# Linear attention on one core: paired output stores, and a regrouped end of the kernel

## The chip, the core and the metric

The kernel runs on one core of a Trainium2 chip. The metric is the device time of one execution in microseconds (us). The kernel before was timed in four runs: 126.88, 127.28, 127.53 and 127.73 us, median 127.4 us. Device work on a core is done by TensorE (PE, with its weight loads shown apart as PEld), VectorE (DVE), ScalarE (ACT), GpSimd (POOL) and SyncE (SP); 16 DMA engines move data between HBM and SBUF, and they are given their work by POOL and SP here.

## What is computed

For each of 8 x 12 = 96 heads, with 512 rows of 64 numbers in float32:

```
Q_feat = max(0, Q) + 1;  K_feat = max(0, K) + 1
KV     = K_feat^T V                    (64 x 64 per head)
K_sum  = sum of K_feat over the rows   (64 per head)
out    = (Q_feat KV) / (Q_feat K_sum + 1e-10)
```

Three inputs of 12 MiB each are read and one output of 12 MiB is written, all in float32.

## The kernel before, in words

**Groups.** The 96 heads are cut into 12 groups of 8 heads (NG = 12, g = 0 to 11). Two groups in a row (0 and 1, 2 and 3, ...) make a pair. A group's output is 1 MiB, 8 KB in each of the 128 partitions. Groups 2 to 9 (`eights(g)`, L93) keep their Q rows in another order than groups 0, 1, 10 and 11: their outputs go to every second of a pair's eight output rows (L137), while the others go to four rows that follow each other. In HBM each partition's piece of one such row is a run of 2 KB, in both cases.

**Loads.** `load` (L104) and `load_q` (L115) are DMAs issued by POOL that read float32 and write bfloat16 into SBUF; `load_pair` (L124) issues K, V and Q of a whole pair, 1 MiB each in SBUF and 2 MiB each in HBM (Q of the last pair in two halves). Each of the three has two buffers (IN_BUFS = 2), so the load of a pair waits until the pair before the last has been used up. The first K goes through SP (L101).

**Work on a group.** `k_features` and `q_features` (DVE, L147) make max(x + 1, 1). `v_blocks` (L158) copies V into a block matrix, three quarters on DVE (L165) and one on ACT (L163). `keys_values` (L177) is 32 matmuls on PE (L184), whose result ACT copies to SBUF (L194, L195). `transposes` (L197) is 16 matmuls on PE into PSUM in two halves (L209); ACT copies each half to SBUF, save the second half of group 11, which DVE copies (L213, L214). `output(g)` (L216) has two halves h = 0 and 1. Each has 16 matmuls (L231) into two PSUM tiles of the pool `psum`, which has two buffers; so the eight matmuls on one tile wait until DVE has used up what lay in it. DVE then takes a reciprocal and one multiplication for each of the two tiles (L241, L242), which writes into the group's tile `o_sb`.

**Stores.** `o_sb` is a tile of one group, of six buffers (OUT_BUFS = 6, 48 KB in each partition). `store(g)` (L134) is one DMA of 1 MiB, issued by POOL, for groups 0 to 9; groups 10 and 11 go out from SP in two DMAs of 512 KB each, one for each half h (L143, L144).

**Order.** The schedule is written out by hand (L260 and on), and each engine does its instructions in that order. The loop over g = 0 to 10 does features, `output(g - 2)`, `keys_values(g)`, and stores group g - 3 (LAG = 3); the transposes of a group lie in its own iteration or the next. `load_pair` stands in the odd iterations 1, 3, 5 and 7, ahead of the store of that iteration. In iteration 10 the order on the engines is `k_features(10)`, `output(8)`, `v_blocks(10)`, `k_features(11)`, `v_blocks(11)`, `keys_values(10)`. After the loop come `q_features(10)`, `transposes(10)`, `q_features(11)`, `output(9)`, `keys_values(11)`, `transposes(11)`, `output(10)`, `output(11)`, and the stores of groups 8 to 11.

POOL's DMAs share eight semaphores in turn. A DMA therefore also waits until the one issued eight before it has landed. POOL and SP issue in order, so a DMA that waits holds back those behind it.

For short, K4 below is the K load of pair 4 (groups 8 and 9), S7 the store of group 7, S10a and S10b the two halves of group 10's, and S45 a store of groups 4 and 5 together.

Of the kernel before, what the change touches and what calls it, by code (L numbers as in the profile page):

```python
# [8 lines left out]
FP32 = mybir.dt.float32  # L9
BF16 = mybir.dt.bfloat16  # L10
ALU = mybir.AluOpType

BANK = 512
IN_BUFS = 2
OUT_BUFS = 6
LAG = 3


# [1 line left out]
def kernel(  # L20
# [21 lines left out]
    nc = tc.nc  # L42

    B, H, S, D = Q.shape
    P = 128
    C = 8
# [3 lines left out]
    NP = 4  # L50
    NG = NPAIR // NP
    D1 = D + 1
    W = 2 * D1

    def view(t, c):
        return t.flatten_outer_dims().rearrange("(n p c) d -> p n c d", p=P, c=c)
# [5 lines left out]
    o_dram = view(out, C)  # L62
# [6 lines left out]
    mid_pool = ctx.enter_context(tc.tile_pool(name="mid", bufs=2))  # L69
    out_pool = ctx.enter_context(tc.tile_pool(name="out_pool", bufs=OUT_BUFS))  # L70
    recip_pool = ctx.enter_context(tc.tile_pool(name="recip", bufs=4))
    psum_kva = ctx.enter_context(tc.tile_pool(name="psum_kva", bufs=2, space=bass.MemoryType.PSUM))
    psum = ctx.enter_context(tc.tile_pool(name="psum", bufs=2, space=bass.MemoryType.PSUM))
# [3 lines left out]
    NV = 4  # L77
# [5 lines left out]
    kva_diag = [kva_all[:, i] for i in range(NV)]  # L83
# [5 lines left out]
    qfs = {}  # L89
    qts = {}  # L90
    outs = {}

    def eights(g):  # L93
        return 2 <= g < NG - 2
# [4 lines left out]
    def load_first_k():  # L99
        k_raw = head_pool.tile([P, 2, C2, D], FP32, name="k_first")  # L100
        nc.sync.dma_start(out=k_raw, in_=k_dram[:, 0:2])  # L101
        raw["k", 0] = k_raw
# [29 lines left out]
                load("q", (g,))  # L132

    def store(g):  # L134
        o_sb = outs.pop(g)
        first = 2 * NP * (g // 2)
        o_to = o_dram[:, first + g % 2 : first + 2 * NP : 2] if eights(g) else o_dram[  # L137
            :, g * NP : g * NP + NP
        ]
        if g < NG - 2:  # L140
            nc.gpsimd.dma_start(out=o_to, in_=o_sb)  # L141
            return
        for h in range(2):  # L143
            nc.sync.dma_start(out=o_to[:, h:NP:2], in_=o_sb[:, h:NP:2])  # L144
# [13 lines left out]
    def v_blocks(g):  # L158
        v_raw = raw.pop(("v", g))
        for b in range(4):  # L160
            ps = slice(32 * b, 32 * b + 32)
            if b == 3:
                nc.scalar.copy(out=v_blk[g % 2][ps, b], in_=v_raw[ps])  # L163
            else:
                nc.vector.tensor_copy(out=v_blk[g % 2][ps, b], in_=v_raw[ps])  # L165
# [11 lines left out]
    def keys_values(g):  # L177
        kf = kfs.pop(g)
        sb = g % 2
        vb = v_all[:, 4 * sb : 4 * sb + 5]  # L180
        kva_ps = psum_kva.tile([P, 5, D], FP32, name="kva_ps")
        for c in range(C2):
            for n in range(2):
                nc.tensor.matmul(  # L184
                    kva_ps[64 * n : 64 * n + 64],
                    lhsT=kf[:, c, n, :],
                    rhs=vb[:, :, n, c, :],
                    start=(c == 0),
                    stop=(c == C2 - 1),
                )  # L190
        kva = kva_diag[g % NV]
        for n in range(2):
            ps = slice(64 * n, 64 * n + 64)
            nc.scalar.copy(out=kva[ps, :, n, 0:D], in_=kva_ps[ps, sb : sb + 4, :])  # L194
            nc.scalar.copy(out=kva[ps, :, n, D], in_=kva_ps[ps, 4 - 4 * sb, 0:4])  # L195

    def transposes(g):  # L197
        qf = qfs.pop(g)
        R, CC = qf.shape[1:3]
        if R == 4 and g % 2:  # L200
            qts[g] = qts[g - 1]
        else:
            qts[g] = mid_pool.tile([P, C, P, R], BF16, name=f"qt{R}")
        first = g % 2 * CC if R == 4 else 0
        for half in range(2):
            qt_ps = psum_qt.tile([P, CC // 2, R, P], BF16, name="qt_ps")
            for c in range(CC // 2):
                for r in range(R):
                    nc.tensor.transpose(  # L209
                        qt_ps[:, c, r], qf[:, r, half * CC // 2 + c, :, :], identity  # L210
                    )
            lo = first + half * CC // 2
            copy = nc.vector.tensor_copy if half and g == NG - 1 else nc.scalar.copy  # L213
            copy(out=qts[g][:, lo : lo + CC // 2], in_=qt_ps.rearrange("p c r q -> p c q r"))  # L214

    def output(g):  # L216
        qt = qts.pop(g)
        o_sb = out_pool.tile([P, NP, C, D], FP32, name="o_sb")
        for h in range(2):
            ops = [psum.tile([P, 2, BANK], FP32, tag="ps", name="o_ps") for _ in range(2)]  # L220
            for c in range(C):
                for j in range(2):
                    if eights(g):
                        b = 2 * (g % 2) + j
                        kva = kva_diag[(g // 2 * 2 + h) % NV]
                        q = slice(16 * (4 * h + b), 16 * (4 * h + b) + 16)
                    else:
                        b = 2 * h + j
                        kva = kva_diag[g % NV]
                        q = slice(32 * b, 32 * b + 32)  # L230
                    nc.tensor.matmul(  # L231
                        ops[c // 4][64 * j : 64 * j + 64, c // 2 % 2, (c % 2) * W : (c % 2) * W + W],
                        lhsT=qt[:, c, q, :],
                        rhs=kva[:, b],
                        start=True,
                        stop=True,
                    )
            for i in range(2):
                cells = ops[i][:, :, 0 : 2 * W].rearrange("p b (c n x) -> p b c n x", n=2, x=D1)
                recip = recip_pool.tile([P, 2, 2, 2, 1], FP32, name="recip")  # L240
                nc.vector.reciprocal(out=recip, in_=cells[:, :, :, :, D:D1])  # L241
                nc.vector.tensor_tensor(  # L242
                    out=o_sb[:, h:NP:2, 4 * i : 4 * i + 4].rearrange(
                        "p n (b c) d -> p b c n d", b=2
                    ),
                    in0=cells[:, :, :, :, 0:D],
                    in1=recip.to_broadcast([P, 2, 2, 2, D]),
                    op=ALU.mult,
                )
        outs[g] = o_sb  # L250

    def clear(first, split, end):
        t = v_all.rearrange("p b m c d -> p (b m c d)").bitcast(FP32)
        w = t.shape[1] // 9
        nc.vector.memset(t[:, first * w : split * w], 0.0)  # L255
        nc.scalar.copy(  # L256
            out=t[:, split * w : end * w], in_=zero.to_broadcast([P, (end - split) * w])
        )

    with tc.manual_schedule():  # L260
        nc.gpsimd.memset(zero, 0.0)
        load_first_k()
        load("v", (0,))
        load("q", (0,))
        for x in "kvq":
            load(x, (1,))
        nc.vector.memset(ones, 0.0)
        for b in range(4):
            nc.vector.memset(ones[32 * b : 32 * b + 32, b : b + 1], 1.0)  # L269
        clear(0, 3, 5)  # L270
        e = v_all[:, 4, :, :, 0:4].rearrange("p n c j -> p (n c) j")
        nc.vector.tensor_copy(out=e, in_=ones[:, None, :].to_broadcast([P, 2 * C2, 4]))
        make_identity(nc, identity)
        nc.gpsimd.memset(kva_all, 0.0)
        load_pair(1)
        clear(5, 7, 9)
        last = NG - 1
        for g in range(last):
            if g and not eights(g - 1):
                transposes(g - 1)  # L280
            elif eights(g) and g % 2:
                transposes(g - 1)
            k_features(g)
            if g < last - 1:
                v_blocks(g)
                if not eights(g):
                    q_features(g)
            if g >= 2:
                output(g - 2)
            if g == last - 1:  # L290
                v_blocks(g)
                k_features(last)
                v_blocks(last)
            if eights(g) and g % 2:
                transposes(g)
            if eights(g) and g % 2 == 0:
                q_features(g)
                q_features(g + 1)
            keys_values(g)
            if g % 2 and g // 2 + 2 < NG // 2:  # L300
                load_pair(g // 2 + 2)
            if g >= LAG:
                store(g - LAG)
        q_features(last - 1)
        transposes(last - 1)
        q_features(last)
        output(last - 2)
        keys_values(last)
        transposes(last)
        output(last - 1)  # L310
        output(last)
        for g in range(last - LAG, NG):
            store(g)
# [30 lines left out]
```

## Time and profile before

| | before |
|---|---|
| median of 4 runs | 127.4 us (126.88 to 127.73) |
| the profiled execution | 126.88 us |
| its span, from the first to the last instruction | 125.1 us |
| busy: DVE | 90.0 us (72% of the span) |
| busy: PE, ACT, POOL | 71.4, 60.4, 26.8 us |
| HBM read and written | 37.75 MB and 12.58 MB, 402 GB/s over the span |
| share of the 16 DMA engines' time: POOL's queue, SP's queue | 97.5%, 6.8% |
| TensorE clock granted, mean | 0.84 |

The profiled execution's own time is 126.88 us and its span 125.1 us; 1.78 us lie outside the span. The page of a profile gives the busy time of each engine, then the span in 40 slices of 3.13 us: a digit is the busy share of an engine in tenths, and the DMA row is the mean busy share of the 16 DMA engines. The row in GB/s counts what is written to the destination. A load writes half of the bytes that it reads, so 210 GB/s in a slice of loads and 420 GB/s in a slice of stores are the same rate on the HBM side. The chain that ended last is followed back from the last instruction. In the list of groups of instructions a row gives line, engine, operation, tiles, count, busy time, mean duration and the idle time ahead of it with what ended it.

### The profile page before, as it was taken

Reading aid. Unit: us, or ns where it says so; the run is one execution under the profiler, and the core shown is the slowest. Engines: PE = TensorE matmul, PEld = TensorE weight load, DVE = VectorE, ACT = ScalarE, POOL = GpSimd, SP = SyncE. Lnnn points to the kernel's source line nnn. Section 1 sums busy time; section 2 is a strip of 40 time slices with the busy share of each in tenths; the row PEclk is TensorE's granted clock in tenths of the full one; section 3 lists DMA queues with packets and bytes.
Section 4 is the critical chain, followed back from the end, with each engine's and each line's share of the span. In section 5 each row is a group of like instructions: output and inputs, shape, how many; then the busy total and the mean of one; then the engine's idle time right before and its main releaser. Section 6 shows DMA issues by size and latency. Waiting matters only on the chain.

```text
span 125.1 us, 2332 instructions
## 1 busy us (share of the span) xinstructions
PE 71.4 (57%) x960; PEld 54.2 (43%) x960; DVE 90.0 (72%) x189; ACT 60.4 (48%) x86; POOL 26.8 (21%) x39
## 2 busy tenths in 40 slices
PE   0004944920696848549594594069787169693720
PEld 0003544810565847438373463056576046472410
DVE  4897280207999899996999930799877996739950
ACT  7832095266009982866729542600895471732000
POOL 6991204000020370224302420203110200020000
PEclk9999997798559999967999959955899756999555
DMA  3999999999999999999999999999999999999993
GB/s 75 342 212 211 212 210 210 212 218 213 208 212 215 216 213 210 210 210 221 245 410 301 210 215 217 210 360 386 221 211 215 208 281 420 423 420 409 389 360 130
DMA packets 12362, 32.12 MB, mean 257 GB/s; under 512 B 576, under 2 KB 576, under 8 KB 12352
## 3 DMA queue, kind: packets, MB, share of 16 engines
q0 software_dynamic: 10992, 28.84, 97.5%
q1 hardware_dynamic: 1360, 3.15, 6.8%
q8 instruction: 7, 0.11, 0.3%
q14 instruction: 3, 0.02, 0.0%
HBM read 37.75 MB, written 12.58 MB: 402 GB/s over the span
## 4 chain that ended last, share of the span: by engine, by line
DMA 47%; DVE 20%; PE 18%; issue 5%; ACT 4%; POOL 2%; POOLq 0%; DVEq 0%
DMA v_raw<-in_V_dram 47%; PE kva_ps L184 12%; DVE o_sb L242 11%; DVE v_all L165 6%; PE qt_ps L209 3%; DVE recip L241 2%; PE o_ps L231 2%; ACT qt L214 2%; ACT v_all L163 2%; POOL v_raw L109 1%; ACT kva_all L194 1%; POOL q_raw L109 1%; DVE qt L214 0%; POOL k_raw L109 0%; ACT kva_all L195 0%
## 5 line engine op out<-in xcount | busy, mean ns | idle before, releaser
L184 PE MATMUL kva_ps<-v_all,kf 128*64 128x320 bf16 x384 | 39.4, 376 | 18.0 <-DVE v_all L165 14.5
L184 PEld LDWEIGHTS <-kf 128*64 128x64 bf16 x384 | 27.9, 139 | 26.2 <-DVE v_all L165 15.6
L231 PE MATMUL o_ps<-kva_all,qt 128*64 128x130 bf16 x384 | 20.2, 243 | 30.3 <-DVE o_sb L242 19.6
L165 DVE COPY v_all<-v_raw 32x2048 bf16<-32x2048 bf16 x36 | 26.2, 727 | 12.8 <-DMA v_raw<-in_V_dram 12.4
L242 DVE TENSOR_TENSOR o_sb<-o_ps,recip 128x512 f32<-128x512 f32 x48 | 33.2, 692 | 1.6
L231 PEld LDWEIGHTS <-qt 128*64 128x64 bf16 x384 | 14.0, 119 | 35.7 <-DVE o_sb L242 23.7
L194 ACT CAST kva_all<-kva_ps 64x256 bf16<-64x256 f32 x24 | 8.9, 371 | 39.5 <-PE kva_ps L184 39.4
L163 ACT COPY v_all<-v_raw 32x2048 bf16<-32x2048 bf16 x12 | 22.6, 1893 | 9.3 <-DMA v_raw<-in_V_dram 9.1
L214 ACT COPY qt<-qt_ps 128x1024 bf16<-128x1024 bf16 x23 | 22.2, 1015 | 3.6 <-PE qt_ps L209 3.3
L141 POOL DMA_DIRECT2D out_dram<-o_sb x10 | 8.3, 834 | 33.6 <-DVE o_sb L242 21.3
L209 PE MATMUL qt_ps<-identity,qf 128*128 128x128 bf16 x192 | 14.9, 240 | 0.0
L147 DVE TENSOR_SCALAR kf<-k_raw 128x1024 bf16<-128x1024 bf16 x22 | 8.6, 433 | 8.4 <-DMA k_raw<-in_K_dram 8.4
L209 PEld LDWEIGHTS <-qf 128*128 128x128 bf16 x192 | 12.7, 108 | 3.2 <-issue 1.7
L241 DVE RECIPROCAL recip<-o_ps 128x8 f32<-128x8 f32 x48 | 9.6, 200 | 3.4 <-PE o_ps L231 3.2
L109 POOL DMA_DIRECT2D k_raw<-in_K_dram x6 | 4.7, 779 | 31.0 <-DVE kf L147 24.7
L147 DVE TENSOR_SCALAR qf<-q_raw 128x1024 bf16<-128x1024 bf16 x24 | 9.0, 432 | 0.3 <-DMA q_raw<-in_Q_dram 0.3
L109 POOL DMA_DIRECT2D v_raw<-in_V_dram x7 | 5.4, 767 | 17.2 <-ACT v_all L163 16.8
L255 DVE MEMSET v_all<- 128x3072 f32 (+1 forms) x2 | 4.4, 2192 | 1.1 <-DVE ones L269 0.7
L195 ACT CAST kva_all<-kva_ps 64x4 bf16<-64x4 f32 x24 | 4.1, 169 | 0.0
L256 ACT COPY v_all<-zero 128x2048 f32<-128x2048 f32 x2 | 3.7, 1894 | 0.0
L109 POOL DMA_DIRECT2D q_raw<-in_Q_dram x4 | 2.9, 722 | 2.3 <-DMA k_raw<-in_K_dram 2.3
L119 POOL DMA_DIRECT2D q_raw<-in_Q_dram x4 | 3.1, 786 | 0.0
(14 smaller groups left out, 7.8 us busy)
## 6 DMA issues: line engine op xcount, KB each, us to landing
out_dram<-o_sb POOLq DMA_DIRECT2D x10, 1024.0 KB, 24.0
k_raw<-in_K_dram POOLq DMA_DIRECT2D x5, 1024.0 KB, 22.4
v_raw<-in_V_dram POOLq DMA_DIRECT2D x5, 1024.0 KB, 23.0
q_raw<-in_Q_dram POOLq DMA_DIRECT2D x4, 1024.0 KB, 26.0
q_raw<-in_Q_dram POOLq DMA_DIRECT2D x4, 512.0 KB, 21.6
out_dram<-o_sb SPq DMA_DIRECT2D x4, 512.0 KB, 3.9
k_first<-in_K_dram SPq DMA_DIRECT2D x1, 1024.0 KB, 5.0
v_raw<-in_V_dram POOLq DMA_DIRECT2D x2, 512.0 KB, 9.5
```

The source lines that it names most:

```text
L109: nc.gpsimd.dma_start(out=bufs[x, s][:, ms], in_=drams[x][:, 2 * groups[0] : 2 * groups[-1] + 2])
L141: nc.gpsimd.dma_start(out=o_to, in_=o_sb)
L147: nc.vector.tensor_scalar(out=dst, in0=src, scalar1=1.0, scalar2=1.0, op0=ALU.add, op1=ALU.max)
L163: nc.scalar.copy(out=v_blk[g % 2][ps, b], in_=v_raw[ps])
L165: nc.vector.tensor_copy(out=v_blk[g % 2][ps, b], in_=v_raw[ps])
L184: nc.tensor.matmul(kva_ps[64 * n : 64 * n + 64], lhsT=kf[:, c, n, :], rhs=vb[:, :, n, c, :], start=(c == 0), stop=(c == C2 - 1),)
L194: nc.scalar.copy(out=kva[ps, :, n, 0:D], in_=kva_ps[ps, sb : sb + 4, :])
L209: nc.tensor.transpose(qt_ps[:, c, r], qf[:, r, half * CC // 2 + c, :, :], identity)
L214: copy(out=qts[g][:, lo : lo + CC // 2], in_=qt_ps.rearrange("p c r q -> p c q r"))
L231: nc.tensor.matmul(ops[c // 4][64 * j : 64 * j + 64, c // 2 % 2, (c % 2) * W : (c % 2) * W + W], lhsT=qt[:, c, q, :], rhs=kva[:, b], start ...
L241: nc.vector.reciprocal(out=recip, in_=cells[:, :, :, :, D:D1])
L242: nc.vector.tensor_tensor(out=o_sb[:, h:NP:2, 4 * i : 4 * i + 4].rearrange("p n (b c) d -> p b c n d", b=2), in0=cells[:, :, :, :, 0:D], i ...
```

## The change

It has two parts.

1. **Stores.** One tile of the output pool now holds a pair: 16 KB in each partition, three buffers (OUT_BUFS = 3), the same 48 KB in all. Groups 0 to 7 are stored two by two, by one DMA of 2 MiB at the place where the odd group's store stood (`store`); the even group's call does nothing. Groups 8 to 11 are stored as before, from their part of a pair's tile. For groups 8 and 9 that part is every second row of the tile.

2. **The end.** `output` is split into `out_matmuls(g, h)` on PE and `norms(g, h)` on DVE. The first half of group 9's output matmuls moves into iteration 10, ahead of `v_blocks(10)`. After the loop, the first half of group 10's output (matmuls and norms) stands between `keys_values(11)` and `transposes(11)`; the second half follows the transposes. ACT makes both copies of group 11's transposes.

For each other group the instructions of an output are what they were.

```diff
-OUT_BUFS = 6
+OUT_BUFS = 3
...
     def store(g):
+        first = 2 * NP * (g // 2)
+        if g < NG - 4:
+            if g % 2:
+                nc.gpsimd.dma_start(
+                    out=o_dram[:, first : first + 2 * NP], in_=outs.pop((g // 2, "pair"))
+                )
+            return
         o_sb = outs.pop(g)
-        first = 2 * NP * (g // 2)
...
-            copy = nc.vector.tensor_copy if half and g == NG - 1 else nc.scalar.copy
-            copy(out=qts[g][:, lo : lo + CC // 2], in_=qt_ps.rearrange("p c r q -> p c q r"))
+            nc.scalar.copy(out=qts[g][:, lo : lo + CC // 2], in_=qt_ps.rearrange("p c r q -> p c q r"))
+
+    def out_matmuls(g, h):
+        if h == 0:
+            open_outputs(g)
+        qt = qts[g]
+        ops = [psum.tile([P, 2, BANK], FP32, tag="ps", name="o_ps") for _ in range(2)]
+        cells_of[g, h] = ops
...
+    def open_outputs(g):
+        if g % 2 == 0:
+            outs[g // 2, "pair"] = out_pool.tile([P, 2 * NP, C, D], FP32, name="o_sb")
+        pair = outs[g // 2, "pair"]
+        o_sb = pair[:, g % 2 : 2 * NP : 2] if eights(g) else pair[:, g % 2 * NP : g % 2 * NP + NP]
+        outs[g] = o_sb
+
+    def norms(g, h):
+        ops = cells_of.pop((g, h))
+        o_sb = outs[g]
...
     def output(g):
...
         for h in range(2):
+            out_matmuls(g, h)
+            norms(g, h)
...
             if g == last - 1:
+                out_matmuls(g - 1, 0)
                 v_blocks(g)
                 k_features(last)
                 v_blocks(last)
...
         q_features(last)
-        output(last - 2)
+        norms(last - 2, 0)
+        out_matmuls(last - 2, 1)
+        norms(last - 2, 1)
         keys_values(last)
+        out_matmuls(last - 1, 0)
+        norms(last - 1, 0)
         transposes(last)
-        output(last - 1)
+        out_matmuls(last - 1, 1)
+        norms(last - 1, 1)
         output(last)
```

The loops of `out_matmuls` and `norms` that are left out are those of `output` before, L221 to L237 and L238 to L249.

More of the change, by code (lines that the diff above doesn't have):

```diff
@@ L91 @@
     outs = {}
+    cells_of = {}
     def eights(g):
@@ L212, in transposes @@
             lo = first + half * CC // 2
-            copy = nc.vector.tensor_copy if half and g == NG - 1 else nc.scalar.copy
-            copy(out=qts[g][:, lo : lo + CC // 2], in_=qt_ps.rearrange("p c r q -> p c q r"))
+            nc.scalar.copy(out=qts[g][:, lo : lo + CC // 2], in_=qt_ps.rearrange("p c r q -> p c q r"))
[5 more added lines that the diff above has]
+        cells_of[g, h] = ops
+        for c in range(C):
+            for j in range(2):
+                if eights(g):
+                    b = 2 * (g % 2) + j
+                    kva = kva_diag[(g // 2 * 2 + h) % NV]
+                    q = slice(16 * (4 * h + b), 16 * (4 * h + b) + 16)
+                else:
+                    b = 2 * h + j
+                    kva = kva_diag[g % NV]
+                    q = slice(32 * b, 32 * b + 32)
+                nc.tensor.matmul(
+                    ops[c // 4][64 * j : 64 * j + 64, c // 2 % 2, (c % 2) * W : (c % 2) * W + W],
+                    lhsT=qt[:, c, q, :],
+                    rhs=kva[:, b],
+                    start=True,
+                    stop=True,
+                )
@@ new lines, in open_outputs @@
+    def open_outputs(g):
[7 more added lines that the diff above has]
+        o_sb = outs[g]
+        for i in range(2):
+            cells = ops[i][:, :, 0 : 2 * W].rearrange("p b (c n x) -> p b c n x", n=2, x=D1)
+            recip = recip_pool.tile([P, 2, 2, 2, 1], FP32, name="recip")
+            nc.vector.reciprocal(out=recip, in_=cells[:, :, :, :, D:D1])
+            nc.vector.tensor_tensor(
+                out=o_sb[:, h:NP:2, 4 * i : 4 * i + 4].rearrange(
+                    "p n (b c) d -> p b c n d", b=2
+                ),
+                in0=cells[:, :, :, :, 0:D],
+                in1=recip.to_broadcast([P, 2, 2, 2, D]),
+                op=ALU.mult,
+            )
@@ L216, in output @@
     def output(g):
-        qt = qts.pop(g)
-        o_sb = out_pool.tile([P, NP, C, D], FP32, name="o_sb")
         for h in range(2):
[L220 to L249, printed above, removed]
@@ L250, in output @@
-        outs[g] = o_sb
+            out_matmuls(g, h)
+            norms(g, h)
     def clear(first, split, end):
```

## The prediction, made before the changed kernel had run

> **What bounds the kernel now.** I read the page's slices first, because they show which engine has no holes.
>
> ```profile
> DVE  4897280207999899996999930799877996739950
> DMA  3999999999999999999999999999999999999993
> GB/s 75 342 212 211 212 210 210 212 218 213 208 212 215 216 213 210 210 210 221 245 410 301 210 215 217 210 360 386 221 211 215 208 281 420 423 420 409 389 360 130
> q0 software_dynamic: 10992, 28.84, 97.5%
> q1 hardware_dynamic: 1360, 3.15, 6.8%
> ```
>
> Every engine has holes but the DMA row: 9 in each slice from the second to the last but one. Where the rate is about 210 GB/s the queue loads (which is 420 on the HBM side), and where it is about 420 it stores. So the time looks like bytes over a rate, with 3 us at the start and 2 at the end. The chain of waits tells another story.
>
> ```profile
> DMA 47%; DVE 20%; PE 18%; issue 5%; ACT 4%; POOL 2%; POOLq 0%; DVEq 0%
> ```
>
> In order of time that chain runs from a V load into PE and DVE at about 79 us, and from there to the end only through compute. It holds because S11b, the last store, is issued the moment DVE has finished. It does not say that the store would have landed earlier if issued earlier. For that I read VectorE's and SP's timelines and the time from issue to landing, one issue at a time.
>
> ```profile
> 107.08 0.21 DVE L241 RECIPROCAL recip<-o_ps 128x8 f32<-128x8 f32 x1 [1.70 <-PE o_ps L231]
> ...
> 112.60 1.22 DVE L214 COPY qt<-qt_ps 128x1024 bf16<-128x1024 bf16 x1 [2.07 <-PE qt_ps L209]
> 113.74 0.20 DVE L241 RECIPROCAL recip<-o_ps 128x8 f32<-128x8 f32 x1
> ...
> 119.94 0.69 DVE L242 TENSOR_TENSOR o_sb<-o_ps,recip 128x512 f32<-128x512 f32 x1
> ```
>
> ```profile
> 115.53 0.38 SPq L144 DMA_DIRECT2D out_dram<-o_sb  x1
> ...
> 120.66 0.37 SPq L144 DMA_DIRECT2D out_dram<-o_sb  x1
> ```
>
> ```profile
> out_dram<-o_sb POOLq DMA_DIRECT2D x1, 1024.0 KB, 8.0
> ...
> out_dram<-o_sb SPq DMA_DIRECT2D x1, 512.0 KB, 4.5
> ...
> out_dram<-o_sb SPq DMA_DIRECT2D x1, 512.0 KB, 3.2
> ```
>
> The last three rows are S9 (issued at 110.82), S10a and S11b. Issue plus landing time, with the same view for the others, gives the landings: S4 106.3, S5 108.8, S6 111.3, S7 113.8, S8 116.3, S9 118.8, S10a 120.0, S10b 121.3, S11a 122.6, S11b 123.8. The step is 2.5 us for 1 MiB and 1.25 to 1.3 for 512 KB, without a gap down to the last one. The time from issue to landing shrinks from 27.0 to 3.2 us: each store waits in the queue, and S11b comes just as the queue runs out. **The DMA queue sets the end; compute reaches it at the same moment.** The last rows to read are stretches of the span; their last two columns are the DMA share and GB/s.
>
> ```profile
> 103.50:116.00 12.50, 9.20 (x146) 6.59 (x142) 8.47 (x20) 4.70 (x11) 0.75 (x1) 0.91 1.02 417
> 116.00:123.00 7.00, 2.60 (x34) 1.64 (x32) 4.46 (x11) 0.00 (x0) 0.00 (x0) 0.50 0.96 373
> 123.00:125.00 2.00, 0.00 (x0) 0.00 (x0) 0.00 (x0) 0.00 (x0) 0.00 (x0) 0.50 0.05 18
> ```
>
> From 116 to 123 us the mean rate falls to 373. The records of the completions say why: each DMA is finished by 16 engines one by one, S8 between 114.40 and 116.27, but S11b between 123.17 and 123.84. The engines that lead by up to 1.9 us wait for work at the end; the one that is last does not.
>
> **Part 2, the end, step by step.** One tile's reciprocal and multiplication start 0.84 us after the ones before (113.74, 114.58, ...); eight of them, groups 10 and 11, take 6.9 us, 113.74 to 120.63.
> - Group 9's first matmuls move ahead of `keys_values(10)`. PE idles for 3.50 us before that (97.7 to 101.2), and they need the PSUM tiles that DVE frees by 98.9; 0.64 us of work is hidden there. DVE's 1.70 us of idle at 107.08 go: it starts on group 9 at 105.4, when `q_features` ends.
> - The second half then runs on PE after `transposes(10)` (106.7), to 107.5. `keys_values(11)` (2.34 us) follows at 107.5 instead of 109.2, to 109.8. Group 10's first half needs 0.65 us more; DVE starts on it at 110.3.
> - `transposes(11)` (1.07 us) end at 111.5. ACT's two copies (1.01 each) end by 113.0; DVE loses its copy (1.22). Group 10's second half reaches DVE at 111.95, and from there six tiles of 0.84 follow without a hole: DVE ends at 117.1 instead of 120.6. S10a, S10b, S11a and S11b are issued at about 112.0, 113.6, 115.4 and 117.1.
> - One wait is new. Group 10's first multiplication writes into the buffer that S45 reads, and so waits for S45 to land: 108.8, where S5 lands now. It is due at 110.5. Behind it on DVE stand the other seven tiles, and all SP stores wait for them. It has 1.7 us to spare, and 3.5 more before it would be later than today. Groups 6 and 8 wait likewise for S01 (lands 69.2) and S23 (88.9); their first multiplications stand at 81.5 and 95.7.
>
> So compute ends 3.5 us earlier. What is late next is the queue: after S9 at 118.8 it holds 2 MiB, at 2.51 us each 123.80, against 123.84 today. **Gain: 0.04 us of the 3.5.** Other ends: nothing, or, if the lost rate of 116 to 123 us could be made up, (417 - 373) / 417 x 7 = 0.7 us.
>
> **Part 1, the stores.** Bytes and HBM runs (2 KB) stay, and so does the order in the queue: K4, V4, Q4, S2, S3, K5, V5, Q5, S4 and on. S0 goes with S1, at about 45.3 rather than 44.5; it lands at 66.7. S23 goes by 59.4 (S3's issue now), S45 by 84.4, S67 at 93.4, S8 at 99.2 as now, S9 at about 108.9. Behind these on POOL stand K4 (issued at 51.6) and K5 (66.8), which wait for other things until then. The queue reaches S2 at about 84, S4 at 103.7, and each store is at least 7 us early. Nothing starves.
>
> What goes is four of 36 DMAs, and 64 of 576 small packets that mark completions, a median of 22 ns each. Per DMA that is 0.02 us on each engine by this price; by landings, two of 512 KB take 2.52 against 2.51 for 1 MiB, 0.01 us. Four times 0.015 makes 0.06 us; ends 0.04 and 0.09.
>
> The packets' shape is not shown for a pair's store or for S8 and S9 from alternate rows. The trace's packets have two prices: 159 ns for 4,096 bytes in POOL's stores, 84 ns for 2,048 in SP's, whose SBUF side is strided. By the second, 10 MiB cost (2 x 84 - 159) x 2,560 / 16 = 1.4 us more; by the landings, which show the same rate for both shapes, nothing. I take nothing, since landings are what the end is made of.
>
> The Trainium skill, "DMA: Bandwidth & Descriptors", section "Anatomy of one DMA", gives each DMA a fixed 2.0 us beside its bytes, and the section "Bandwidth" advises 1 MiB or more. If the four removed DMAs each paid that in series, an estimate by that page would be 8 us of gain. The spacing above speaks against it in a queue that is never empty, where the fixed part of one DMA lies under its neighbours.
>
> **Sum.** 126.88 - 0.04 - 0.06 = 126.8 us for the profiled execution, the lowest of the four runs. The median lies 0.5 above it; the same 0.1 from 127.4 gives **127.3 us**.
>
> **Rivals.**
> - *Lost rate made up (126.7 or less, chance 0.12).* With the SP stores issued early, all 16 engines stay fed, and the engines that trail might get a larger share of the rate. That gives the 0.7 us above. For it: the rate does fall from 417 to 373. Against: trailing engines step 1.25 us per 512 KB whether the leaders idle or not.
> - *The chain is right (123.9, chance 0.02).* If S11b waited for nothing but its issue, 3.5 us go. Against: landings without a gap.
> - *Dearer packets (128.8, chance 0.09), the slower side.* The pair tile makes POOL's stores go out in 2,048-byte packets at 84 ns. Since the queue never empties, it decides from the first packet, and its 1.4 us go to the end in full. For it: S8 and S9 do get a strided SBUF side. Against: the landings of SP's stores. With only S8 and S9 hit it is 0.28 us, inside the forecast's range.
> - *It does nothing (127.4, chance 0.10).* Part 1 changes neither order nor bytes, and part 2 is hidden whole; this is 0.1 from my forecast, and on the same side of the bound.
>
> **How the numbers follow.** A measurement of this kernel tells about 0.5% (0.64 us) from no change. Forecast 0.67. Runs before spread by 0.4 about the median, which I add to the forecast: 126.9 to 127.7. To leave out no more than 0.2 and take in the 0.7 of gain and half of the 1.4, the range is 126.5 to 128.0. Chances: faster 0.14 (0.12 + 0.02), slower 0.09, same 0.77 (0.67 + 0.10).
>
> **What the profile after would show.** DVE's last multiplication ending near 117.1, without the two idles; SP's last issue near 117.1 and landing near 123.8, so some 6.7 us after issue in place of 3.2; 10 POOL stores become 6; packets fall by 64; the DMA row stays at 9; span about 125.0. The forecast is wrong if S11b lands before 123.2, if the step per MiB differs from 2.5 us, or if the DMA row shows a hole.

## The result, and the profile after

The changed kernel takes 127.49 us (median of 53 runs, 126.99 to 128.34), the kernel before 127.18 us beside it (79 runs, 126.72 to 128.01). The ratio is 1.0023 with a 95% interval of 1.0013 to 1.0032: 0.3 us slower, where 0.1 us less was forecast. The time lies in the range, and within the 0.5% that was called no change; the sign is wrong. The range was wide enough for either sign, so that it holds says nothing for the mechanism.

The profiled execution took 128.09 us with a span of 126.0, so it is one of the longer ones, 0.6 above the median. The page's rows for the DMAs, and its chain:

```profile
DMA  3999999999999999999999999999999999999992
GB/s 82 330 209 214 210 210 210 213 217 216 205 213 211 218 211 211 213 213 218 264 406 276 198 211 217 217 373 372 201 186 214 211 267 419 419 416 413 408 391 94
DMA packets 12298, 32.12 MB, mean 255 GB/s; under 512 B 512, under 2 KB 512, under 8 KB 12288
...
DMA 51%; DVE 18%; PE 13%; ACT 6%; issue 4%; POOL 1%; POOLq 0%; DVEq 0%
```

The DMA row has no hole. Three slices of loads fall short of the usual 210: 198, right behind the first pair's store, and 201 and 186 behind the second. VectorE's and SP's timelines and the landings at the end:

```profile
106.25 0.20 DVE L259 RECIPROCAL recip<-o_ps 128x8 f32<-128x8 f32 x1
...
111.38 0.21 DVE L259 RECIPROCAL recip<-o_ps 128x8 f32<-128x8 f32 x1 [0.85 <-PE o_ps L238]
...
117.50 0.69 DVE L260 TENSOR_TENSOR o_sb<-o_ps,recip 128x512 f32<-128x512 f32 x1
```

```profile
113.19 0.38 SPq L151 DMA_DIRECT2D out_dram<-o_sb  x1
...
118.22 0.37 SPq L151 DMA_DIRECT2D out_dram<-o_sb  x1
```

```profile
out_dram<-o_sb POOLq DMA_DIRECT2D x1, 1024.0 KB, 10.7
...
out_dram<-o_sb SPq DMA_DIRECT2D x1, 512.0 KB, 7.9
...
out_dram<-o_sb SPq DMA_DIRECT2D x1, 512.0 KB, 6.9
```

DVE ends at 118.2 instead of 120.6, S11b is issued at 118.22 instead of 120.66, and lands 6.9 us later, at 125.1, instead of 3.2 us later at 123.8. Compute is out of the way, and the end is later all the same. The last stretches of the span say that the end itself runs well:

```profile
103.50:116.00 12.50, 10.94 (x160) 8.42 (x156) 10.53 (x26) 5.90 (x13) 0.75 (x1) 0.81 1.02 415
116.00:123.00 7.00, 0.57 (x14) 0.25 (x8) 2.13 (x5) 0.00 (x0) 0.00 (x0) 0.67 1.02 401
123.00:126.00 3.00, 0.00 (x0) 0.00 (x0) 0.00 (x0) 0.00 (x0) 0.00 (x0) 0.50 0.23 87
```

From 116 to 123 us the rate is 401 instead of 373. What is left over for 123 to 126 was already late at 104: the last load, Q5, had landed at 105.0 instead of 103.7. So I looked where the time was lost before that, in the two stretches of loads that follow stores. First the kernel before, then the changed one; the last two columns are the DMA share and GB/s.

```profile
68.00:74.00 6.00, 3.85 (x46) 2.87 (x48) 4.02 (x11) 4.14 (x4) 1.44 (x2) 0.79 1.13 213
...
88.00:94.00 6.00, 4.77 (x82) 4.14 (x84) 4.65 (x11) 5.89 (x9) 0.62 (x1) 0.96 1.12 214
94.00:98.00 4.00, 2.49 (x50) 2.02 (x46) 3.12 (x9) 1.61 (x5) 0.13 (x1) 1.00 1.12 212
```

```profile
68.00:74.00 6.00, 3.48 (x38) 2.77 (x40) 4.38 (x10) 4.56 (x5) 2.15 (x3) 0.72 1.11 207
...
88.00:94.00 6.00, 4.55 (x82) 3.96 (x82) 4.17 (x10) 5.91 (x9) 0.90 (x1) 1.00 1.11 195
94.00:98.00 4.00, 2.44 (x50) 1.98 (x45) 3.24 (x9) 1.57 (x5) 0.00 (x0) 1.00 1.12 212
```

At 88 to 94 us 19 GB/s of 214 are missing, 0.5 us of work, and at 68 to 74 us 0.2 us; from 94 us on the rates are equal again. In the trace's packet records, load packets that take 173 ns elsewhere take 415 to 1,170 ns at 70.5 to 70.9 and at 90.4 to 91.9 us, one to three us after the queue has turned from S01 and S23 to loads. In the first profile of before no load packet is over 400 ns there.

These stretches are not the whole delay of this execution. A DMA has landed when the last of the 16 engines has finished its part. By the last engine K4 and K5 land 0.3 us later than before, V5 1.3 us later, and S11b 1.3 us later. At V5 fifteen engines finish between 97.46 and 99.05 us, as a block, and the sixteenth at 100.01. In between, at 96.3 us, the records hold a packet of 16,384 bytes and 961 ns on the instruction queue; before has one of 974 ns at 96.4 us, and there V5 is not held up. The records do not name the engine of a packet, but 0.96 us on one engine is the size of that packet. So about 1.0 of the 1.3 us looks like the chance of which engine it met, and an execution 0.6 us over the median is a poor witness for a loss of 0.3.

A measure that is less open to such chance is the mean, over the 16 DMA engines, of a DMA's completion. By it the plain stretches of loads are equal in eleven profiles of both kernels and the variants below that keep the queue's order (K4 to Q4 9.85 to 9.89 us, K5 to Q5's end 9.98 to 10.02). They differ at the turns from stores to loads:

| us, mean completion | Q3 to K4 (over S0, S1) | Q4 to K5 (over S2, S3) |
|---|---|---|
| without a turn: 2 x 2.51 + 4.94 | 9.96 | 9.96 |
| before, and before again | 10.17, 10.20 | 10.00, 10.03 |
| end alone; pairs late | 10.36; 10.26 | 10.02; 10.01 |
| changed, and changed again | 10.50, 10.29 | 10.58, 10.19 |
| pairs alone; pairs early (second) | 10.50; 10.41 | 10.26; 10.05 |
| pairs early (first) | 10.39 | 10.18 |
| pair tile only; pair in halves | 10.61; 10.27 | 10.20; 10.07 |

By the last engine, which sets the end, the two kinds of turn differ less. The four profiles in the rows "changed" and "pairs alone" take 10.40 and 10.14 us on average, the four in the rows "before" and "end alone" 10.27 and 10.14.

Theory A: part 1, the pair's stores, makes the turn from a store to loads dearer. Theory B: part 2, the end with both queues (POOL's and SP's) full, costs. A third reading, that the packets of 500 ns and more were one execution's chance, was tested with them.

### The profile page after: what moved, and what is told of

Read it like the earlier page. It is cut to its first block, busy times and chain, and to the rows that moved or that the text cites. A ratio compares the mean times of both kernels' runs of the same rounds, so it can differ in the third digit from the quotient of the medians.

```text
span 126.0 us, 2325 instructions
## 1 busy us (share of the span) xinstructions
PE 71.2 (56%) x960; PEld 54.8 (43%) x960; DVE 88.0 (70%) x188; ACT 61.3 (49%) x87; POOL 23.6 (19%) x35
## 2 busy tenths in 40 slices
DMA packets 12298, 32.12 MB, mean 255 GB/s; under 512 B 512, under 2 KB 512, under 8 KB 12288
## 4 chain that ended last, share of the span: by engine, by line
DMA 51%; DVE 18%; PE 13%; ACT 6%; issue 4%; POOL 1%; POOLq 0%; DVEq 0%
DMA v_raw<-in_V_dram 51%; PE kva_ps L191 10%; DVE o_sb L260 8%; DVE v_all L172 7%; ACT v_all L170 3%; PE qt_ps L216 2%; DVE recip L259 2%; ACT qt L220 2%; DVE qf L154 1%; PE o_ps L238 1%; ACT kva_all L201 1%; POOL v_raw L110 1%; POOL q_raw L110 1%; DVE kf L154 1%; ACT kva_all L202 0%
## 5 line engine op out<-in xcount | busy, mean ns | idle before, releaser
L191 PE MATMUL kva_ps<-v_all,kf 128*64 128x320 bf16 x384 | 39.9, 379 | 18.1 <-DVE v_all L172 13.8
L191 PEld LDWEIGHTS <-kf 128*64 128x64 bf16 x384 | 28.6, 140 | 26.3 <-DVE v_all L172 15.4
L238 PE MATMUL o_ps<-kva_all,qt 128*64 128x130 bf16 x384 | 19.0, 233 | 27.7 <-DVE o_sb L260 16.5
L238 PEld LDWEIGHTS <-qt 128*64 128x64 bf16 x384 | 13.3, 114 | 32.6 <-DVE o_sb L260 19.9
L220 ACT COPY qt<-qt_ps 128x1024 bf16<-128x1024 bf16 x24 | 23.1, 1015 | 3.2 <-PE qt_ps L216 2.8
L216 PE MATMUL qt_ps<-identity,qf 128*128 128x128 bf16 x192 | 15.4, 244 | 0.0
L139 POOL DMA_DIRECT2D out_dram<-o_sb x4 | 3.8, 938 | 19.1 <-DVE o_sb L260 17.9
L148 POOL DMA_DIRECT2D out_dram<-o_sb x2 | 1.5, 759 | 16.1 <-DVE o_sb L260 16.1
L110 POOL DMA_DIRECT2D q_raw<-in_Q_dram x4 | 2.9, 728 | 0.0
```

What stands on the lines that cost most here:

```text
L110: nc.gpsimd.dma_start(out=bufs[x, s][:, ms], in_=drams[x][:, 2 * groups[0] : 2 * groups[-1] + 2])
L191: nc.tensor.matmul(kva_ps[64 * n : 64 * n + 64], lhsT=kf[:, c, n, :], rhs=vb[:, :, n, c, :], start=(c == 0), stop=(c == C2 - 1),)
L216: nc.tensor.transpose(qt_ps[:, c, r], qf[:, r, half * CC // 2 + c, :, :], identity)
L220: nc.scalar.copy(out=qts[g][:, lo : lo + CC // 2], in_=qt_ps.rearrange("p c r q -> p c q r"))
L238: nc.tensor.matmul(ops[c // 4][64 * j : 64 * j + 64, c // 2 % 2, (c % 2) * W : (c % 2) * W + W], lhsT=qt[:, c, q, :], rhs=kva[:, b], start ...
```

## The experiments

Ratios are against the kernel before on the same chip, with a 95% interval.

**The two parts, and both kernels again.** Four runs, the first two with one part of the change each.

```diff
 pairs_alone: the changed kernel, with the order of before at the end
-                out_matmuls(g - 1, 0)
...
-        norms(last - 2, 0)
-        out_matmuls(last - 2, 1)
-        norms(last - 2, 1)
+        output(last - 2)
...
 end_alone: the changed kernel, with a tile and a store for each group
-OUT_BUFS = 3
+OUT_BUFS = 6
...
+        outs[g] = out_pool.tile([P, NP, C, D], FP32, name="o_sb")
```

> Part 1 alone: groups 0 to 7 stored two by two from tiles of a pair, and the end as before. Theory A (the pair tiles and stores cost it): all of the 0.3 us is here, ratio 1.0015 to 1.0035, and the profile shows queue time lost between 60 and 100 us, where two pair stores and the loads behind them run. Theory B (the regrouped end costs it): ratio 0.998 to 1.001, and each 1 MiB of store lands 2.5 us after the one before.

> Part 2 alone: one store and one tile for each group as before, and the regrouped end. Theory A: ratio 0.999 to 1.0005, DVE ends some 3 us earlier and the last store lands when it did. Theory B (with both queues full in the last 10 us, or SP's stores issued early, the DMA engines do less): ratio 1.0015 to 1.0035, and from S8's landing to the last landing more than the 7.57 us of before.

> The changed kernel once more, to see which marks of its profile come back. Both theories: ratio 1.001 to 1.0035. If the packets of 500 to 1,170 ns near 70.5 and 91 us belong to the pair stores, they are here again behind each of the two pair stores that loads follow; if they were one execution's, they are gone and the ratio stays.

> The kernel before, against itself: both theories ratio 0.999 to 1.001, which says how small a difference five rounds can tell. Its profile says what a second execution does to the landings: the lead of the first over the last of 16 engines was 1.9 us in the first; theory A has no packets over 400 ns near 70 and 90 us here.

Pairs alone: 127.66 us, ratio 1.0029 (1.0008 to 1.0050). End alone: 127.10, 1.0005 (0.9985 to 1.0024). Both again: 127.59, 1.0027 (1.0010 to 1.0044). Before against itself: 1.0014 (0.9995 to 1.0032), which warns that one set of five rounds tells 0.15% from nothing only just. Three sets with the pair's stores (the first measurement among them) and none without lie clear of 1: A is favoured, and B is not needed, though the interval of end alone reaches 1.0024. The slow load packets come back behind pair stores (both turns in pairs alone, the second in both again), but end alone shows them too, behind S1 at 70.4 us, and pair tile only below shows ten of them behind S1. So they belong to turns and are not the pair's stores' own.

In end alone the last multiplication is

```profile
116.47 0.69 DVE L250 TENSOR_TENSOR o_sb<-o_ps,recip 128x512 f32<-128x512 f32 x1
```

and DVE ends at 117.16, 3.5 us before 120.63, for no gain that shows.

**DMAs alone.** Is the pattern of the DMAs enough? These kernels leave out all computation and store zeros.

```diff
+        for step in range(STEPS):
+            s = step % 6
+            for x, dram in (("k", k_dram), ("v", v_dram)):
+                t = in_pool.tile([P, 4, C2, D], BF16, name=f"{x}_raw")
+                nc.gpsimd.dma_start(out=t, in_=dram[:, 4 * s : 4 * s + 4])
+            t = in_pool.tile([P, 2, C4, D], BF16, name="q_raw")
+            nc.gpsimd.dma_start(out=t, in_=q_eights[:, 2 * s : 2 * s + 2])
+            stores(s)
...
+        if STORE == "pair":
+            nc.gpsimd.dma_start(out=to, in_=pair)
+        for i in range(2):
+            if STORE == "singles":
+                nc.gpsimd.dma_start(out=to[:, i:8:2], in_=singles[i])
+            if STORE == "halves":
+                nc.gpsimd.dma_start(out=to[:, 4 * i : 4 * i + 4], in_=pair[:, 4 * i : 4 * i + 4])
+            if STORE == "alternate":
+                nc.gpsimd.dma_start(out=to[:, i:8:2], in_=pair[:, i:8:2])
```

> DMAs alone, with no computation: 24 steps, each with the K, V and Q loads of a pair (1 MiB each in SBUF) and the store of a pair's 2 MiB of zeros, all on POOL's queue, which never empties. Here the store is two DMAs of 1 MiB, every second output row each, from two tiles of 8 KB in a partition, as in the kernel before. 8 MiB at some 2.5 us each make 20 us for a step, some 480 us in all. This is the base for the other three; each has 24 places where a store is followed by a load, against two in the kernel.

> DMAs alone; the store is one DMA of 2 MiB from a tile of 16 KB in a partition, as in the changed kernel. If the DMAs' pattern alone costs the changed kernel its 0.3 us at two such places, 0.15 us each, this is 24 x 0.15 = 3.6 us longer than the base. If the cost needs the other engines at work, or the place of the store's issue, it is within 1 us of the base.

> DMAs alone; the store is two DMAs of 1 MiB from the pair's tile, the first four output rows and the last four. If the size of one DMA (2 MiB) is the cost, within 1 us of the base; if the order in which output rows are written is, as long as the pair's single DMA.

> DMAs alone; the store is two DMAs of 1 MiB with the base's output rows (every second one each), but out of the pair's tile, so that the SBUF side has a stride as the stores of groups 8 and 9 have in the changed kernel. If a strided SBUF side costs, longer than the base, by at most 24 x 2 x 0.14 = 6.7 us (the dearer packets of the prediction); if only the HBM side counts, within 1 us of the base.

Measured: singles 487.05 us, pair 487.50, halves 487.18, alternate 486.76, each from four runs with a spread of up to 3.2 us. All are within 0.5 us of the base, 0.02 us for each of 24 turns. By their forecasts this said that the pattern alone costs nothing, and that tiles or other engines were needed. But the profiles showed one thing amiss with the test: the slow load packets stood mostly at the first few turns, while the completions of the first and the last engine had drifted 3.5 to 4.2 us apart by the end. In the kernel they are 1.2 to 2.3 us apart at the turns (3.2 in one profile). At the second and third turn of the test, with the engines 1.5 to 2.6 us apart, the turn takes 10.31 and 10.38 us by mean completion with a pair's store and 9.97 to 10.23 with the others. I came back to that below.

**Which stores, and which property of them.** Four variants of pairs alone.

```diff
 pairs_early, with 4 <= g < 8 for pairs_late; the other groups have tiles of one_pool (four)
-        if g < NG - 4:
+        if g < 4:
...
 pair_tile_only: no store of a pair
-        if g < NG - 4:
-            if g % 2:
-                nc.gpsimd.dma_start(
-                    out=o_dram[:, first : first + 2 * NP], in_=outs.pop((g // 2, "pair"))
-                )
-            return
...
 pair_in_halves:
+                pair = outs.pop((g // 2, "pair"))
+                for i in range(2):
+                    nc.gpsimd.dma_start(
+                        out=o_dram[:, first + NP * i : first + NP * i + NP],
+                        in_=pair[:, NP * i : NP * i + NP],
+                    )
```

> The kernel before, with pair tiles and one DMA of 2 MiB for groups 0 to 3 alone; groups 4 to 11 have a tile and a store each. These are the two pair stores behind which the queue goes back to loads. Theory A1 (the cost arises where a pair's store is followed by loads): ratio 1.0015 to 1.0035 and 0.2 to 0.6 us more than before from the mean landing of Q3 to that of K4 and from Q4 to K5 together. Rival A2 (every pair store or every pair tile costs): about half, 1.0005 to 1.0015.

> The kernel before, with pair tiles and one DMA of 2 MiB for groups 4 to 7 alone; behind these two only stores follow. Theory A1: ratio 0.999 to 1.0005. Rival A2: about half of the change's cost, 1.0005 to 1.0015, and more than 5.03 us for a pair's store.

> The kernel before, with tiles of a pair but one store of 1 MiB for each group, where and in the HBM order it was. If DVE's writes at a stride of 4 KB, or DMA reads at that stride, cost the 0.3 us: ratio 1.0015 to 1.0035. If the single DMA of 2 MiB does: 0.999 to 1.0005.

> Pair tiles, and where the pair's store stood two DMAs of 1 MiB in a row, output rows 0 to 3 and 4 to 7. If the size of one DMA is the cost: ratio 0.999 to 1.0005. If the place of the issue or the order of output rows in HBM is: 1.0015 to 1.0035.

Pairs early took 137.1 us in five runs and 139.3 and 139.5 in two, and its time told nothing of the question: I had given it four tiles of a group for eight groups, so group 8 waited for S4 to land.

```profile
108.30 0.69 DVE L265 TENSOR_TENSOR o_one<-o_ps,recip 128x512 f32<-128x512 f32 x1 [11.70 <-DMA out_dram<-o_one]
```

That wait of 11.7 us stands in the run of 139.25 us; the queue then ran dry (10 and 5 GB/s in two slices of 3.4 us), and the median is 9.9 us above before. Its two turns come ahead of the wait and are in the table. Pairs late: 127.24 us, 1.0008 (0.9985 to 1.0032). Pair tile only: 127.35, 1.0007 (0.9987 to 1.0028). Pair in halves: 127.57, 1.0019 (0.9993 to 1.0044). The medians go the way of theory A1, which is A narrowed: a single DMA of a pair costs where loads follow it, and the tile costs nothing. But each interval holds both forecasts. In pairs late the landings agree with A1 too: S45 and S67 take 5.07 and 5.04 us by mean completion, and before has 5.09 and 5.03 for the same bytes in single stores. In pair tile only the turns took 10.61 and 10.20 us in its one profile, though its S0 and S1 are the DMAs of before: a turn differs by some 0.4 us from one execution to the next, and single profiles can't settle this. More turns were needed, with the engines nearly in step.

**The turn by itself.** DMAs alone again, 24 steps, with the four ways to store. Each step begins with a load into the tile of the last step's last load, and so waits until that has landed.

```diff
+            nc.gpsimd.dma_start(out=k_tile, in_=k_dram[:, 4 * s : 4 * s + 4])
+            stores(s)
+            nc.gpsimd.dma_start(out=v_tile, in_=k_dram[:, 4 * t : 4 * t + 4])
+            nc.gpsimd.dma_start(out=k_tile, in_=v_dram[:, 4 * t : 4 * t + 4])
```

> DMAs alone, 24 steps; a step loads 1 MiB (in SBUF), stores a pair, loads twice 1 MiB, and the next step waits until all of it has landed, so that the 16 engines turn from storing to loading nearly together. Here two stores of 1 MiB from two tiles, every second row each, as before. Three loads at 4.95, two stores at 2.5 and some 3 us of waiting make 23 us for a step, some 550 us in all; base for the other three.

> The same with one store of 2 MiB from the pair's tile. If a pair's store makes the turn dearer by 0.15 to 0.25 us, as the two turns in the kernel's landings have it, 3.6 to 6 us longer than the base. If the turn's cost is chance, within 1.5 us of it.

> The same with two stores of 1 MiB from the pair's tile, rows 0 to 3 and 4 to 7. If the size of one DMA makes the turn dearer, as the base; if the order of the rows in HBM does, as the pair's store.

> The same with two stores of 1 MiB of every second row each, out of the pair's tile. If the strided SBUF side makes the turn dearer, longer than the base; if only the size of a DMA or the order of rows counts, as the base.

| | median us (4 runs) | over singles, per turn | first load to load behind the store, last engine | first to last engine at the store |
|---|---|---|---|---|
| singles | 609.90 (605.82 to 610.49) | | 10.68 us | 1.06 us |
| alternate | 608.93 (608.49 to 610.24) | -0.04 us | 10.59 us | 1.08 us |
| halves | 614.65 (612.62 to 617.85) | +0.20 us | 10.97 us | 1.31 us |
| pair | 619.90 (618.20 to 621.65) | +0.42 us | 11.13 us | 2.00 us |

The last two columns are from one profile each, that of halves from its longest run. Steps were longer than I had put them (25 us, not 23), about the same in all four. The DMA issues, sizes and median time to landing, of singles and of pair:

```profile
out_dram<-o_single POOLq DMA_DIRECT2D x48, 1024.0 KB, 11.5
...
v_tile<-in_K_dram POOLq DMA_DIRECT2D x24, 1024.0 KB, 17.5
```

```profile
out_dram<-o_pair POOLq DMA_DIRECT2D x24, 2048.0 KB, 15.0
...
v_tile<-in_K_dram POOLq DMA_DIRECT2D x24, 1024.0 KB, 18.7
```

The load behind the store takes 1.2 us longer to land, counted from its issue; up to 0.6 us of that is its earlier issue (one store's issue of 0.91 us ahead of it instead of two of 0.76). The ranges of singles and pair lie apart by 7.7 us, so a pair's store costs here, with the DMAs alone, without tiles being written or computation. Alternate is no dearer than singles: the SBUF side is not it. Halves have the pair's rows in the pair's tile and two DMAs of 1 MiB: by the runs the order of the rows in HBM makes about half of the cost, having all in one DMA the other half.

The landings say where this time lies, as means over the 24 steps of one profile each:

| us | first load to end of store, last engine (mean engine) | end of store to load behind it, last engine (mean engine) | sum, mean engine |
|---|---|---|---|
| singles | 5.89 (5.86) | 4.79 (4.50) | 10.36 |
| alternate | 5.83 (5.83) | 4.76 (4.52) | 10.35 |
| halves | 5.94 (5.80) | 5.03 (4.75) | 10.55 |
| pair | 6.48 (6.01) | 4.65 (4.51) | 10.53 |

The pair's extra time is in the store itself, not in the load behind it, and most of it by the last engine alone: the mean engine loses 0.17 us of the 0.45. The halves' extra time is in the load. The packet records agree: store packets over 300 ns (159 is usual) number 124, 97, 431 and 593 in the order of the first table, load packets over 300 ns (173 is usual) 1,840, 1,823, 1,742 and 1,659. Each step of this test ends with a wait for the last engine, so it pays for engines that fall apart in every step. The kernel has no such wait at its turns, and what it pays for need not be the same.

**Back to the kernel, and a version with fewer turns.** The last two runs.

```diff
 pairs_early2: as pairs_early, but the four tiles of a group are for groups 4 to 7 alone
+        if 4 <= g < 8:
+            outs[g] = one_pool.tile([P, NP, C, D], FP32, name="o_one")
...
 one_turn: the kernel before, with
-OUT_BUFS = 6
+OUT_BUFS = 8
...
-            if g >= LAG:
-                store(g - LAG)
+            if g == 5:
+                store(0)
+                store(1)
+            if g == 7:
+                store(2)
+                store(3)
+            if g >= 7:
+                store(g - LAG)
```

> The kernel before, with one DMA of 2 MiB for groups 0 and 1 and for 2 and 3 alone, both followed by loads; groups 4 to 11 have a store of 1 MiB each (four tiles of a group for groups 4 to 7, tiles of a pair for the others). Theory A1 (the cost arises where a pair's store is followed by loads): ratio 1.001 to 1.0035, against 1.0008 for the run with pair stores for groups 4 to 7 alone. Rival A2 (every pair store costs): half of the change's cost, about 1.001, the same as that run.

> The kernel before with the stores of groups 0 and 1 issued behind the loads of pair 4 and those of groups 2 and 3 behind the loads of pair 5 (eight tiles of a group instead of six): the queue turns from stores to loads once instead of twice. If a turn costs what the landings of before show (10.17 from Q3 to K4 and 10.00 from Q4 to K5, against 2 x 2.51 + 4.94 = 9.96 without one): 0.05 to 0.2 us less, ratio 0.9985 to 0.9995. Rival: turns of single stores cost nothing that five rounds can tell, ratio 0.999 to 1.001.

Pairs early, without the wait: 127.69 us, 1.0044 (1.0018 to 1.0070), against 1.0008 (0.9985 to 1.0032) for pairs late. Theory A1 holds by the medians, but barely clear of the noise: the two ratios differ by 0.0036, and the uncertainty of that difference, from their half-widths of 0.0026 and 0.0024, is 0.0035. The stores' packets go the same way: in the turn over S0 and S1, 31 to 40 store packets were more than 40 ns over the usual in the five profiles with one DMA for this pair (both of pairs early counted), and 16 to 24 in the six others. In the turn over S2 and S3 the counts overlap (3 to 13 and 2 to 7).

Taken together, the four sets with a pair's store ahead of loads lie at 1.0023, 1.0027, 1.0029 and 1.0044, each clear of 1. The four sets with single stores there, in the order of before (before again, end alone, pairs late, pair tile only), lie at 1.0005 to 1.0014, none clear of 1.

One turn was meant as the version that beats both. It took 127.50 us, 1.0026 (1.0003 to 1.0048): slower, and my forecast was wrong. By mean completion its one turn (S0 and S1, then K5) took 10.37 us, and the turn that it removed, over S2 and S3, had cost only 10.02 against 9.96. So there was next to nothing to gain at the turn that went. A reading that fits, from one profile, is that it counts which stores stand ahead of the loads, not how many turns there are: S0 and S1 are rows 0 to 3 and 4 to 7, as in halves, S2 and S3 every second row. The loss of 0.3 us, without any pair's store, is not explained. In its profile the mean completion of the last store is that of before (123.42 and 123.39), and the last engine's is 0.75 us later. A store of groups 0 and 1 by every second row was not tried.

## Why the prediction was wrong, step by step

- **What bounds the kernel** held. Compute ended 2.4 us earlier (3.5 in end alone), and no time was gained that shows.
- **Part 2** held as a whole: 1.0005 (0.9985 to 1.0024), forecast -0.04 us. DVE's end was put at 117.1 and was 117.16 in end alone; in the changed kernel's profile it was 118.2, as V5 landed 1.3 us later and DVE waited for it (the two lines below, before and changed). S45 landed at 110.1 instead of 108.8, and the first multiplication that waits for it stood at 111.6, not held up. The lost rate of 116 to 123 us was made up (401), which brought nothing: the leading engines no longer idle there, and the trailing one sets the end.

```profile
98.83 2.32 DVE L165 COPY v_all<-v_raw 32x2048 bf16<-32x2048 bf16 x3
...
100.04 2.08 DVE L172 COPY v_all<-v_raw 32x2048 bf16<-32x2048 bf16 x3 [1.16 <-DMA v_raw<-in_V_dram]
```

- **Part 1 failed at its packets step**: "I take nothing, since landings are what the end is made of." The landings used there, one store behind another from 106 us on, have no turn in them, and there a pair's store shows no cost (pairs late 1.0008, and 5.07 and 5.04 us for its two). Part 1 as a whole costs 0.3 us by the runs: the term -0.06 should have been about +0.3. Where it costs is less sure. By mean completion the two turns behind S01 and S23 carry it: means of four profiles each, 10.43 against 10.25 and 10.27 against 10.02, 0.4 us together. With pair tile only and the first pairs early counted too, it is 0.3, and single profiles of the same stores differ by as much. By the last engine the two turns differ by 0.1 us. The turn stood in the profile of before (10.17 and 10.00 against 9.96), and I had not looked at it.
- **The signs of being wrong** were the wrong ones. S11b landed at 125.1, not before 123.2; S45 and S67 kept the step of 2.5 us per MiB (5.04 and 5.01 us for 2 MiB each), and S9 alone took longer (3.7 us), with SP's stores beside it; the DMA row has no hole. A loss in the stretches of loads was not among them.
- **"Bytes and HBM runs (2 KB) stay, and so does the order in the queue"** is true and was not enough: rows 0 to 7 in one DMA for every second row in two is another order of writes. In the test of the turn by itself the order alone cost 0.20 us (halves), with the same bytes and runs.
- The rival *dearer packets* had the right part and sign, and the wrong cause. The packets did not change shape (11,776 of 2 to 8 KB in both profiles, 12,352 less 576 and 12,288 less 512; 64 small ones fewer, as forecast), and its 1.4 us did not come.
- The Trainium skill, "DMA: Bandwidth & Descriptors", section "Bandwidth", advises DMAs of 1 MiB or more. Here 2 MiB in one DMA was dearer than 1 MiB in two, by 0.2 us at a turn (pair against halves, 24 turns, each with a wait for the last engine); by the mean engine the two were alike (10.53 and 10.55).

What the kernel's cost is made of stays open. The turn by itself gives 0.42 us for S23 against every second row, and 0.2 for S01 against the halves that S0 and S1 are: 0.6 us, twice the measured. By the mean engine it gives 0.17 and nothing. The test has the engines 0.8 us apart at the load ahead of the store, and the kernel 1.1 to 2.1 us (3.2 in one profile); at up to 4 us apart the cost was 0.02. That the distance decides is an inference; the wait in each step of the one test, which the other lacks, is a rival that was not separated from it. Why writes in this order cost was not tried.

## What to carry to other kernels

When a queue is never empty, price a change to its DMAs in the place where they stand. Landings of one store behind another say nothing of a store behind which loads follow. Read a DMA's landing both by the mean of its 16 engines and by the last: the mean shows a loss that all engines share, the last sets the end, and a single execution can lose 1 us on one engine by chance. A benchmark of DMAs alone that waits for the last engine in each step pays for the engines' distance each time, where the kernel pays once. Freeing an engine that meets the queue only at the end brought nothing here, for 3.5 us freed.

## What was not expected of the hardware

- By mean completion a turn to stores and back to loads costs 0.04 to 0.65 us beside the bytes, and differs by some 0.4 us between profiles with the same stores (10.17 in before, 10.61 in pair tile only), where stretches of loads agree to 0.04 us over 10 us.
- The 16 DMA engines drift apart in steps, and stay apart while the queue is full: completions of one DMA were 0.4 us apart until 23 us and 1.2 us apart at 28 us in before, and 1.9 us from 65 us on. At 26.4 us the records hold a 16,384-byte packet of 893 ns on the instruction queue. Where such a packet seems to have met the last engine, the end is later even if the mean does not move: in both again the mean completion of the last store is 0.15 us earlier than in before (123.24 and 123.39), the last engine's 1.15 us later, and 1.1 us of that came at S67, behind a packet of 1,007 ns at 110.5 us. In all twelve profiles of the kernel and its variants the device time is 2.9 to 3.1 us above the last landing.
- In a full queue one more DMA costs about 0.01 us (by the last engine two stores of 512 KB take 2.52 us, one of 1 MiB 2.51).
